# A gated linear recurrence whose next block's projection, convolution and split come ahead of the preceding block's scans, and whose gate products come together

## The chip, the cores and the metric

The kernel runs on one core of one Trainium2 chip. The metric is the device time of one execution in microseconds (us); several runs are taken and their median is compared.

## What is computed

The reference is one layer of an encoder trunk with four parallel branches, applied to two sequences (prompt and sample) of 1024 tokens and 1024 channels. Everything is float32. The change touches one branch, a gated linear recurrence (LRU) over 512 channels, in four blocks of 128. Cut to that branch:

```python
def rglru_branch(u, gate, conv_w, conv_b, w_a, b_a, w_x, b_x, lam):
    xc = centred_dwconv(u.astype(f32), conv_w.astype(f32)) + conv_b.astype(f32)
    xb = xc.reshape(bsz, L, LRU_BLOCKS, LRU_BLOCK_W)
    for d, rev in enumerate((False, True)):
        r = jax.nn.sigmoid(jnp.einsum('blhi,hij->blhj', xb, w_a[d].astype(f32)).reshape(bsz, L, LRU_W) + b_a[d].astype(f32))
        i = jax.nn.sigmoid(jnp.einsum('blhi,hij->blhj', xb, w_x[d].astype(f32)).reshape(bsz, L, LRU_W) + b_x[d].astype(f32))
        log_a = -LRU_C * jax.nn.softplus(-lam[d].astype(f32)) * r
        drive = jnp.sqrt(-jnp.expm1(2.0 * log_a)) * (i * xc)
        _, h = lax.associative_scan(_linear_combine, (jnp.exp(log_a), drive), axis=1, reverse=rev)
        hs.append(h)
    return ((hs[0] + hs[1]) * jax.nn.silu(gate.astype(f32))).astype(u.dtype)
```

u and gate are columns of one input projection of the normalised input. The other branches are a gated linear attention (GLA), a gated delta rule (DeltaNet), in which a lower triangular matrix I + L is inverted for each head and direction, and a diagonal state space model (S5). Each branch's output is projected, weighed with a sigmoid gate of the input ("merge gate") and added; an output projection and a norm close the layer.

## The kernel before

Tiles are channel-major: 128 channels on the partitions, 1024 tokens along a row. A float32 product is made of three passes over exact splits: each operand is a hi and a lo part, the hi a cast on ScalarE, the lo a subtraction on GpSimd, and TensorE computes hi x hi, hi x lo and lo x hi. A projection of 128 columns is two halves of 512 tokens, each 8 x 3 = 24 matmuls of 128x512 into a PSUM bank of the kind pj.

Each sequence passes through stages: the DeltaNet projections, then the **LRU stage**, then GLA and S5, then the DeltaNet recurrence with the merge, then the output projection. In the LRU stage three kinds of work are emitted side by side by `weave`, which spreads each generator evenly over its number of steps: `cor`, the inverses of I + L for two pairs of heads (`dn_core1`, 30 steps), `lru`, the four LRU blocks (16 steps), and some ten merge gates (`early`, tile fg); in sequence 0 also the rotations of S5 (tiles E and rot). The eight PSUM banks are cut into pj=3, lr=2 (the LRU's gate products) and dn=3 (DeltaNet). A scheduler of the framework then orders each engine's instructions by priority, close to the order of emission; each engine takes its own in that order and waits for semaphores.

An LRU block (`lru_block`) goes: projection into the tile up, convolution by four VectorE steps over 128x1024 into xc, cast xh (ScalarE), remainder xl (GpSimd), split of the gate weights, half of the block's silu gate (tile sg) as cover, then for each direction d two gates r and i, each two halves of three matmuls into an lr bank that a sigmoid on ScalarE empties; i x xc on GpSimd; exp, tanh and square on ScalarE; a VectorE step on r, a square root, a product i x r and the scan of 128x1024 on VectorE. Both directions share nothing but xc; r, i and sg have two buffers each. The next block's projection is emitted when the scans of the block before have been.

`dn_core1` builds L (tiles sl and rl: additions on VectorE, an exp on ScalarE, products with k k^T), writes its 32x32 diagonal blocks to DRAM (lan_d), reads them back one block per partition, and inverts them by 31 steps of two VectorE instructions (tm, then sl): here called the **lane solve**. The result goes through lan_d again, and 64- and 128-wide products on TensorE (tile dn) put the blocks together. There are two solves in each sequence, one per pair of heads; the stage's first half holds the first, its second half the other.

Every instruction is issued by a small helper and so has the same line, L54, in the profile: go by the tiles' names.

Of the kernel before, what the change touches and what calls it, by code (L numbers as in the profile page):

```python
# [17 lines left out]
T = 1024  # L18
# [15 lines left out]
def tile_hybrid_trunk(ctx: ExitStack, tc: tile.TileContext, A):  # L34
# [10 lines left out]
    class Line:  # L45
        """an engine that, while line[0] is set, takes its work in the order of the program"""
# [32 lines left out]
    def weave(*gens):  # L79
        """emit generators side by side, each spread evenly over its number of steps"""  # L80
# [8 lines left out]
    def after(i, j):  # L89
        """of one engine's instructions, i goes after j"""  # L90
# [35 lines left out]
    # ---------------------------------------------------------------- constants  # L126
# [5 lines left out]
    # ------------------------------------------------------- small helpers (DVE)  # L132
# [73 lines left out]
    def wcols(wp, src, k0, kt, c0, m):  # L206
        """columns c0:c0+m of rows 128 * (k0:k0+kt): list over k of (hi, lo) [128, m]"""
# [12 lines left out]
    def mm3_steps(out, ws, xs):  # L220
        """out[m, n] = sum_k w[k].T x[k], three float32r passes of the exact split; a step for each k"""
# [24 lines left out]
    # DRAM scratch  # L246
# [12 lines left out]
    # ================================================================ sequences  # L259
# [41 lines left out]
    def proj_tok(xn, wp, src, c0, toks, evac):  # L301
        """token-major: out[tok, 256 cols]"""
# [13 lines left out]
    def gate_steps(xn, wp, c0, out):  # L316
        """out = silu(projection block)"""
# [28 lines left out]
        # columns 0:48 the hi, 64:112 the lo part: one pass of the hi of xn carries both  # L346
# [25 lines left out]
    # ----------------------------------------------------------------- DeltaNet  # L372
# [1286 lines left out]
```

## Time and profile before

| | us |
|---|---|
| median of 3 runs | 3234.07 (3233.86 to 3234.88) |
| profiled execution, its span | 3238.6 |
| TensorE busy in it | 2991.5 (92%) |
| VectorE busy | 1986.7 (61%) |
| ScalarE busy | 1250.0 (39%) |
| GpSimd busy | 1077.0 (33%) |

The span is the profiled execution's time from its first instruction to its last; no other time of that execution is known, and it is one execution. Busy time counts instructions that run, so what is left of the span is an engine's idle time. "Clock" is the share of its full clock, 2.4 GHz, that TensorE was granted. A row of the form "PE lr <- ACT xh" says that a matmul into a tile lr waited for ScalarE's result xh.

### The profile page before, as it was taken

The numbers are of one execution on the slowest core, as the hardware profiler recorded it, in microseconds if no ns is written. First come the engines' busy times: TensorE is split into PE (matmuls) and PEld (weight loads), VectorE is DVE, ScalarE is ACT, GpSimd is POOL, SyncE is SP. The second block draws the span as 40 slices with busy tenths as digits, with TensorE's granted clock in tenths as the row PEclk, the third lists the DMA queues.
The fourth block names the chain that finished last, engine by engine and source line by source line (L and its number), as shares of the span: only waits on it lengthen the run. The fifth ranks groups of instructions, "written<-read, shape, count | busy, mean of one in ns | idle before, by whom it ended". The sixth has DMA issues, their size and how long they took to land. (4 is left out here: it accounts for less than half of the span.)

```text
span 3238.6 us, 42921 instructions
## 1 busy us (share of the span) xinstructions
PE 2991.5 (92%) x15642; PEld 2490.3 (77%) x15642; DVE 1986.7 (61%) x3941; ACT 1250.0 (39%) x1948; POOL 1077.0 (33%) x851
## 2 busy tenths in 40 slices
PE   6898879899899999999999988989989999999998
PEld 4666667779798787778778866777879788788877
DVE  6998885721767556565655367672266744656645
ACT  4333555532323244332254355652232324433223
POOL 2267643421334223111343333442133422321123
PEclk9999889999999999999999998999999999999999
DMA  5234525331323346654453342533123334565343
GB/s 106 93 131 141 175 78 160 92 121 27 91 85 108 115 142 195 199 195 127 160 174 112 104 129 81 157 88 121 40 79 99 109 101 158 182 205 184 114 151 124
DMA packets 397812, 409.04 MB, mean 126 GB/s; under 512 B 93184, under 2 KB 290848, under 8 KB 397600
## 3 DMA queue, kind: packets, MB, share of 16 engines
q1 hardware_dynamic: 397600, 406.29, 40.3%
q8 instruction: 123, 2.02, 0.3%
q14 instruction: 89, 0.73, 0.1%
HBM read 298.48 MB, written 107.71 MB: 125 GB/s over the span
## 5 line engine op out<-in xcount | busy, mean ns | idle before, releaser
L54 PE MATMUL pj<-xn,hi 128*128 128x512 f32 x4352 | 1402.0, 402 | 19.8 <-DVE misc L54 4.3
L54 POOL TENSOR_TENSOR lo<-raw,hi 128x512 fp32r<-128x512 f32 x432 | 612.9, 1423 | 1529.3 <-ACT hi L54 1405.6
L54 PEld LDWEIGHTS pj<-xn,hi 128*128 128x128 f32 x4352 | 824.0, 192 | 205.4 <-issue 15.2
L54 PE MATMUL pj<-xn,lo 128*128 128x512 f32 x2176 | 868.4, 399 | 2.4 <-POOL lo L54 2.4
L54 ACT CAST hi<-raw 128x512 fp32r<-128x512 f32 x432 | 264.7, 618 | 785.3 <-PE pj L54 512.6
L54 PEld LDWEIGHTS pj<-xn,lo 128*128 128x128 f32 x2176 | 417.8, 192 | 100.7 <-issue 7.4
L54 ACT ACT_TABLE_LOAD x184 | 236.1, 1283 | 96.8 <-DVE Ab L54 50.4
L54 PE MATMUL pj<-hi,xn 128*128 128x256 f32 x1024 | 263.1, 346 | 3.4 <-DVE vt L54 3.4
L54 PE MATMUL pj<-yh,hi 128*128 128x512 f32 x576 | 237.4, 412 | 5.1 <-DVE mg L54 3.9
L54 PEld LDWEIGHTS pj<-hi,xn 128*128 128x128 f32 x1024 | 230.3, 266 | 4.2 <-DVE vt L54 3.8
L54 PE MATMUL pj<-yh,lo 128*128 128x512 f32 x576 | 226.0, 392 | 0.0
L54 PE MATMUL pj<-yl,hi 128*128 128x512 f32 x576 | 225.4, 391 | 0.4 <-DVE yl L54 0.4
L54 PE MATMUL pj<-lo,xn 128*128 128x256 f32 x512 | 176.4, 347 | 0.0
L54 DVE TENSOR_TENSOR sg<-sg,pj 128x512 f32<-128x512 f32 x128 | 87.5, 684 | 100.8 <-PE pj L54 83.0
L54 PEld LDWEIGHTS pj<-lo,xn 128*128 128x128 f32 x512 | 135.3, 266 | 0.4
L54 PE MATMUL pj<-hi,mh 128*128 128x512 f32 x384 | 124.0, 399 | 7.0 <-ACT mh L54 4.1
L54 PEld LDWEIGHTS pj<-yh,hi 128*128 128x128 f32 x576 | 109.0, 189 | 24.6 <-DVE mg L54 4.5
L54 PEld LDWEIGHTS pj<-yh,lo 128*128 128x128 f32 x576 | 108.4, 188 | 23.8
L54 PEld LDWEIGHTS pj<-yl,hi 128*128 128x128 f32 x576 | 109.1, 189 | 19.2 <-DVE yl L54 1.1
L54 ACT ACTIVATE fg<-pj,bmg 128x512 f32<-128x512 f32 x112 | 76.6, 686 | 81.9 <-PE pj L54 47.3
L54 DVE TENSOR_TENSOR_SCAN w<-E,v 64x512 f32<-64x512 f32 x64 | 100.3, 1568 | 0.9
L54 DVE TENSOR_TENSOR yl<-yr,yh 128x512 fp32r<-128x512 f32 x80 | 60.3, 763 | 63.2 <-ACT yh L54 62.9
(380 smaller groups left out, 4608.8 us busy)
## 6 DMA issues: line engine op xcount, KB each, us to landing
raw<-in_w_in_dram SPq DMA_DIRECT2D x176, 256.0 KB, 2.9
raw<-in_w_merge_gate_dram SPq DMA_DIRECT2D x128, 256.0 KB, 3.3
sl<-rows_d SPq DMA_DIRECT2D x128, 256.0 KB, 6.6
gs_d<-fg SPq DMA_DIRECT2D x112, 256.0 KB, 3.3
sg<-gs_d SPq DMA_DIRECT2D x112, 256.0 KB, 2.9
sl<-qkv_d SPq DMA_DIRECT2D x40, 512.0 KB, 5.0
raw<-in_w_branch_dram SPq DMA_DIRECT2D x64, 256.0 KB, 3.4
yr<-ysp SPq DMA_DIRECT2D x64, 256.0 KB, 3.1
```

What stands on the lines that cost most here:

```text
L54: i = f(*a, **kw)
```

## The change

`lru_block` becomes `lru_all`, one generator for all four blocks, in three parts. `front(b)` is a block's projection, convolution and split, now by halves of 512 tokens, and its gate weights. `products(b)` makes all eight gate tiles of a block (two directions, r and i, two halves) one after the other, and the two products i x xc. `scans(b)` holds the block's silu gate, and for each direction exp, tanh, square, square root and scan. They are emitted as front 0, then for each b: products b, front b + 1, scans b. The square gets a tile of its own (a2; it lay in up), sg has one buffer, and the weave counts 18.4 steps for the LRU. `conv` takes its width from its output. All else in the diff is removed comments.

```diff
     def conv(out, up, cw, bias=None):
+        n = out.shape[1]
         if bias is None:
-            ts(V, out, up[:, 0:T], cw[:, 0:1], None, ALU.mult)
+            ts(V, out, up[:, 0:n], cw[:, 0:1], None, ALU.mult)
         else:
-            ts(V, out, up[:, 0:T], cw[:, 0:1], bias, ALU.mult, ALU.add)
+            ts(V, out, up[:, 0:n], cw[:, 0:1], bias, ALU.mult, ALU.add)
         for j in range(1, 4):
-            stt(out, up[:, j:j + T], cw[:, j:j + 1], out, ALU.mult, ALU.add)
+            stt(out, up[:, j:j + n], cw[:, j:j + 1], out, ALU.mult, ALU.add)
...
-    def lru_block(s, b, xn, wp, pl):
...
+    def lru_all(s, xn, wp, pl):
+        two = ("r", "i")
         wt = lambda shape, tag, dt=F32: pl.tile(shape, dt, tag=tag, name=nm(tag), bufs=2 if tag in two else 1)
+        def front(b):
+            up = wt([128, T + 4], "up")
+            conv_in(xn, wp, up, LRU_X + b * 128)
+            yield 1
+            xc = wt([128, T], "xc")
+            xh, xl = wt([128, T], "xh", F32R), wt([128, T], "xl", F32R)
+            cb = lru_cb[:, b:b + 1]
+            for sl in HALVES:
+                conv(xc[:, sl], up[:, sl.start:sl.stop + 3], lru_cw[:, b], cb)
+                S.copy(xh[:, sl], xc[:, sl])
+                tt(G, xl[:, sl], xc[:, sl], xh[:, sl].bitcast(F32), ALU.subtract)
...
+            hi, lo = split_tile(pl, 512, srcs, 512, "lw", 1, 1)
+            return xc, xh, xl, hi, lo
+        def products(b, xc, xh, xl, hi, lo):
+            r, ig = ([wt([128, T], t_) for _ in range(2)] for t_ in two)
+            for d in range(2):
+                for gi, (dst, bias) in enumerate(((r[d], lru_ba), (ig[d], lru_bx))):
+                    mi = slice((gi * 2 + d) * 128, (gi * 2 + d + 1) * 128)
+                    for sl in HALVES:
+                        p = bank("lr")
+                        for n, (a, x) in enumerate(((hi, xh), (hi, xl), (lo, xh))):
+                            mm(p, a[:, mi], x[:, sl], start=(n == 0), stop=(n == 2))
+                        act(dst[:, sl], p, AF.Sigmoid, bias=bias[:, d, b:b + 1])
                     yield 0.4
+                tt(G, ig[d], ig[d], xc, ALU.mult)
+            return r, ig
+        def scans(b, r, ig):
+            sg = wt([128, T], "sg")
+            gate = gate_steps(xn, wp, LRU_G + b * 128, sg)
...
+            half()
+            for d in range(2):
+                j = d * 4 + b
+                a = wt([128, T], "a")
+                act(a, r[d], AF.Exp, scale=sp8n[:, j:j + 1])
+                act(r[d], r[d], AF.Tanh, scale=sp8[:, j:j + 1])
+                a2 = wt([128, T], "a2")
...
+                half()
+                if d == 0:
+                    yield 1
+            run(gate)
+            tt(G, ig[0], ig[0], ig[1], ALU.add)
+            tt(V, sg, ig[0], sg, ALU.mult)
+            put_y(sg, s, 0, b)
+            yield 1
+        new = yield from front(0)
+        for b in range(4):
+            got = yield from products(b, *new)
+            if b < 3:
+                new = yield from front(b + 1)
+            yield from scans(b, *got)
...
-                lru = chain(*(lru_block(s, b, xn, wp, pl) for b in range(4)))
+                lru = lru_all(s, xn, wp, pl)
                 cor = chain(*(dn_core1(s, p, pr, cpl) for p in range(2)))
-                todo = [(30, cor), (16, lru), *early(s, NP[s][2], 0.15, xn, wp, fp)]
+                todo = [(30, cor), (18.4, lru), *early(s, NP[s][2], 0.15, xn, wp, fp)]
```

The rows that follow are the engines' orders of instructions. On TensorE, sequence 0, before the change: pj468 and pj470 belong to merge gates (before pj468 stand the two halves of block 0's gate, 24 matmuls each), lr432 and lr433 are the first gate products of block 0.

```order
L54 MATMUL pj468_3277<-xn0_6_98,hi466_3272 128x512 x2
L54 MATMUL pj468_3277<-xn0_6_98,lo467_3273 128x512
L54 MATMUL pj468_3277<-xn0_7_99,hi466_3272 128x512 x2
L54 MATMUL lr432_3097<-xh416_3025,hi419_3030 128x512
L54 MATMUL lr433_3102<-xh416_3025,hi419_3030 128x512
L54 MATMUL pj468_3277<-xn0_7_99,lo467_3273 128x512
L54 MATMUL pj470_3305<-xn0_0_92,hi463_3266 128x512 x2
L54 MATMUL pj470_3305<-xn0_0_92,lo464_3267 128x512
L54 MATMUL pj470_3305<-xn0_1_93,hi463_3266 128x512 x2
```

After the change, the same place: pj464 and pj465 are the two halves of block 1's projection, lr425 is block 0's first product.

```order
L54 MATMUL pj464_3233<-xn0_7_99,hi462_3228 128x512 x2
L54 MATMUL pj464_3233<-xn0_7_99,lo463_3229 128x512
L54 MATMUL pj465_3259<-xn0_0_92,hi459_3222 128x512 x2
L54 MATMUL pj465_3259<-xn0_0_92,lo460_3223 128x512
L54 MATMUL pj465_3259<-xn0_1_93,hi459_3222 128x512 x2
L54 MATMUL pj465_3259<-xn0_1_93,lo460_3223 128x512
L54 MATMUL lr425_3046<-xh416_3021,hi419_3036 128x512
L54 MATMUL pj465_3259<-xn0_2_94,hi459_3222 128x512 x2
L54 MATMUL pj465_3259<-xn0_2_94,lo460_3223 128x512
L54 MATMUL pj465_3259<-xn0_3_95,hi459_3222 128x512 x2
L54 MATMUL lr425_3046<-xl417_3022,hi419_3036 128x512
L54 MATMUL lr425_3046<-xh416_3021,lo420_3037 128x512
```

The first product has moved up: 30 matmuls of block 1's projection stand between block 0's projection (and eight dn products) and it, where 24 of each of two gate halves and 23 of a merge gate stood. Block 1's projection is now here instead of behind the scans.

On VectorE, sequence 0, before: xc566 is block 1's convolution, sl477 and tm are the lane solve (the 13th to 15th of its 31 steps are among these rows), i484 is block 0's scan, sg421 its output.

```order
L54 TENSOR_TENSOR tm529_3622<-sl476_3363,sl477_3364 128x247
L54 TENSOR_TENSOR E881_5525<-E881_5525,tm894_5572 128x4x64
L54 TENSOR_TENSOR sl477_3364<-sl477_3364,tm529_3622 128x13x19
L54 TENSOR_TENSOR tm530_3625<-sl476_3363,sl477_3364 128x252
L54 TENSOR_SCALAR xc566_3785<-up520_3555,lru_cw_407,lru_cb_412 128x1024
L54 TENSOR_TENSOR sl477_3364<-sl477_3364,tm530_3625 128x14x18
L54 TENSOR_TENSOR sg421_3036<-i454_3220,sg421_3036 128x1024
L54 SCALAR_TENSOR_TENSOR xc566_3785<-up520_3555,lru_cw_407,xc566_3785 128x1024
L54 TENSOR_TENSOR tm531_3628<-sl476_3363,sl477_3364 128x255
L54 SCALAR_TENSOR_TENSOR xc566_3785<-up520_3555,lru_cw_407,xc566_3785 128x1024
L54 TENSOR_TENSOR sl477_3364<-sl477_3364,tm531_3628 128x15x17
L54 SCALAR_TENSOR_TENSOR xc566_3785<-up520_3555,lru_cw_407,xc566_3785 128x1024
```

After: xc477 is block 1's convolution, in halves; i424 is the product i x r and the scan of block 0's second direction; sl495 and tm are the solve (its 6th and 7th step).

```order
L54 TENSOR_TENSOR tm501_3488<-sl494_3468,sl495_3469 128x156
L54 TENSOR_SCALAR xc477_3372<-up457_3218,lru_cw_407,lru_cb_412 128x512 x2
L54 TENSOR_TENSOR i424_3045<-i424_3045,r422_3043 128x1024
L54 TENSOR_TENSOR sl495_3469<-sl495_3469,tm501_3488 128x6x26
L54 SCALAR_TENSOR_TENSOR xc477_3372<-up457_3218,lru_cw_407,xc477_3372 128x512 x2
L54 SCALAR_TENSOR_TENSOR i424_3045<-a533_3636,i424_3045 128x1024
L54 TENSOR_TENSOR tm527_3618<-sl494_3468,sl495_3469 128x175
L54 SCALAR_TENSOR_TENSOR xc477_3372<-up457_3218,lru_cw_407,xc477_3372 128x512
L54 TENSOR_TENSOR tm886_5531<-E881_5516,rot_512 128x4x4
L54 SCALAR_TENSOR_TENSOR xc477_3372<-up457_3218,lru_cw_407,xc477_3372 128x512
L54 TENSOR_TENSOR sl495_3469<-sl495_3469,tm527_3618 128x7x25
L54 SCALAR_TENSOR_TENSOR xc477_3372<-up457_3218,lru_cw_407,xc477_3372 128x512
```

The convolution of block 1 has moved from the middle of the solve to its beginning, and lies in pieces between its steps.

On ScalarE, sequence 1, block 0, before: sl2805 is an exp of L, r2800 the first direction's r from the banks lr2801 and lr2802, a2811 the exp of the recurrence behind it.

```order
L54 ACTIVATE r2800_16045<-lr2801_16046,lru_ba_414 128x512
L54 ACT_TABLE_LOAD
L54 ACTIVATE sl2805_16087<-sl2805_16087 128x1024
L54 ACT_TABLE_LOAD
L54 ACTIVATE r2800_16045<-lr2802_16051,lru_ba_414 128x512
L54 ACT_TABLE_LOAD
L54 ACTIVATE a2811_16123<-r2800_16045,sp8n_503 128x1024
```

After: sl2803 and sl2808 are exps of L; i2792, r2790 and r2791 are sigmoids that empty banks (r2791 belongs to the second direction).

```order
L54 ACT_TABLE_LOAD
L54 ACTIVATE sl2808_16108<-sl2808_16108 128x1024
L54 ACT_TABLE_LOAD
L54 ACTIVATE i2792_16017<-lr2799_16056,lru_bx_417 128x512
L54 ACT_TABLE_LOAD
L54 ACTIVATE r2790_16015<-r2790_16015 128x1024
L54 ACT_TABLE_LOAD
L54 ACTIVATE r2791_16016<-lr2800_16062,lru_ba_414 128x512
```

The sigmoids that empty the banks now stand with an exp of L ahead of them, which waits for VectorE, and with four table loads and the first direction's square root (the row that reads and writes r2790) among them.

## Rows read from the trace of the kernel before

**Rows 1.** The page: its head and TensorE's busy time.

```profile
span 3238.6 us, 42921 instructions
...
PE 2991.5 (92%) x15642; PEld 2490.3 (77%) x15642; DVE 1986.7 (61%) x3941; ACT 1250.0 (39%) x1948; POOL 1077.0 (33%) x851
```

**Rows 2.** Windows of the two LRU stretches: busy us and instructions, clock, DMA.

```profile
334.00:720.00 386.00, 340.06 (x1832) 273.17 (x1833) 256.42 (x485) 198.26 (x275) 164.33 (x165) 0.92 0.42 127
...
1886.00:2251.00 365.00, 326.11 (x1778) 261.34 (x1778) 232.51 (x401) 195.62 (x268) 133.21 (x93) 0.93 0.40 121
```

**Rows 3.** TensorE's waits, 334 to 720 us: total us, times, longest.

```profile
PE lr L54 <- ACT xh L54: 17.9, 3, 7.1
...
PE dn L54 <- DMA sl<-lan_d: 6.7, 2, 4.9
...
PE lr L54 <- ACT r L54: 5.9, 2, 3.1
...
PE lr L54 <- POOL xl L54: 3.3, 2, 1.8
```

**Rows 4.** TensorE's waits, 1886 to 2251 us.

```profile
PE lr L54 <- ACT xh L54: 10.5, 2, 5.9
...
PE dn L54 <- DMA sl<-lan_d: 6.2, 2, 4.8
...
PE lr L54 <- ACT i L54: 5.2, 1, 5.2
...
PE lr L54 <- ACT r L54: 4.7, 1, 4.7
...
PE lr L54 <- POOL xl L54: 3.6, 2, 1.9
```

**Rows 5.** Timeline, TensorE, products behind a wait: start, duration, operation, [idle before].

```profile
552.40 0.50 PE L54 MATMUL lr<-xh,hi 128*128 128x512 f32 x1 [3.06 <-ACT r L54]
...
614.46 0.79 PE L54 MATMUL lr<-xh,hi 128*128 128x512 f32 x1 [5.20 <-ACT xh L54]
...
617.02 0.80 PE L54 MATMUL lr<-xl,hi 128*128 128x512 f32 x1 [1.77 <-POOL xl L54]
...
2147.95 0.80 PE L54 MATMUL lr<-xh,hi 128*128 128x512 f32 x1 [5.94 <-ACT xh L54]
...
2150.50 0.80 PE L54 MATMUL lr<-xl,hi 128*128 128x512 f32 x1 [1.76 <-POOL xl L54]
```

**Rows 6.** Windows behind two waits, and one at full clock.

```profile
552.00:557.00 5.00, 4.60 (x13) 3.64 (x14) 0.00 (x0) 4.94 (x6) 0.00 (x0) 0.66 0.33 105
...
614.40:621.60 7.20, 5.38 (x12) 3.95 (x13) 6.99 (x7) 4.82 (x9) 5.36 (x3) 0.50 0.22 71
...
621.80:629.00 7.20, 7.20 (x33) 5.83 (x32) 6.82 (x12) 6.46 (x8) 2.63 (x2) 1.00 0.14 37
```

**Rows 7.** Windows of the lane solves in the first halves.

```profile
354.60:462.00 107.40, 87.98 (x368) 71.07 (x367) 102.98 (x202) 61.47 (x71) 54.30 (x68) 0.89 0.43 127
...
1955.80:2007.00 51.20, 44.80 (x182) 35.84 (x180) 49.36 (x74) 22.24 (x28) 19.91 (x13) 0.90 0.23 69
```

**Rows 8.** Instructions of tile i: min/median/max ns, first and last start.

```profile
L54 POOL TENSOR_TENSOR i<-i,xc x16: 2358/2400/2923, 395.5 to 2186.2; 128x1024 f32<-128x1024 f32 x16
...
L54 DVE TENSOR_TENSOR i<-i,r x16: 1182/1225/2258, 398.7 to 2191.8; 128x1024 f32<-128x1024 f32 x16
...
L54 DVE TENSOR_TENSOR_SCAN i<-a,i x16: 2269/2292/3266, 399.9 to 2193.5; 128x1024 f32<-128x1024 f32 x16
```

**Rows 9.** Instructions of tile xc: a convolution step.

```profile
L54 DVE SCALAR_TENSOR_TENSOR xc<-up,lru_cw,xc x24: 1269/1279/1293, 362.8 to 2145.5; 128x1024 f32<-128x1024 f32 x24
```

**Rows 10.** Timeline at 614 us: lane solve on VectorE, subtraction on GpSimd.

```profile
614.33 0.42 DVE L54 TENSOR_TENSOR sl<-sl,tm 128x252 f32<-128x252 f32 x1
...
614.48 2.48 POOL L54 TENSOR_TENSOR xl<-xc,xh 128x1024 fp32r<-128x1024 f32 x1 [17.45 <-ACT xh L54]
...
614.78 2.55 DVE L54 TENSOR_TENSOR tm<-sl,sl 128x247 f32<-128x247 f32 x1
```

More of the change, by code (lines that the diff above doesn't have):

```diff
@@ L798, in norm_out @@
         put_y(y, *dst)
-    def lru_block(s, b, xn, wp, pl):
-        two = ("r", "i", "sg")
+    def lru_all(s, xn, wp, pl):
+        two = ("r", "i")
         wt = lambda shape, tag, dt=F32: pl.tile(shape, dt, tag=tag, name=nm(tag), bufs=2 if tag in two else 1)
-        up = wt([128, T + 4], "up")
-        conv_in(xn, wp, up, LRU_X + b * 128)
-        yield
-        xc = wt([128, T], "xc")
-        conv(xc, up, lru_cw[:, b], lru_cb[:, b:b + 1])
-        xh, xl = wt([128, T], "xh", F32R), wt([128, T], "xl", F32R)
-        S.copy(xh, xc)
-        tt(G, xl, xc, xh.bitcast(F32), ALU.subtract)
-        def srcs(raw):
-            v = raw[:, :512].rearrange("p (a d c) -> p a d c", a=2, d=2)
-            yield v[:, 0], A["lru_w_a"][0, :, b].rearrange("d i j -> i d j")
-            yield v[:, 1], A["lru_w_x"][0, :, b].rearrange("d i j -> i d j")
-        hi, lo = split_tile(pl, 512, srcs, 512, "lw", 1, 1)
-        sg = wt([128, T], "sg")
-        gate = gate_steps(xn, wp, LRU_G + b * 128, sg)
-        def half():
-            for _ in range(8):
-                next(gate, None)
-        half()
-        yield 0.4
-        hv = []
-        for d in range(2):
-            gts = []
-            for gi, bias in ((0, lru_ba), (1, lru_bx)):
-                r = wt([128, T], ("r", "i")[gi])
-                mi = slice((gi * 2 + d) * 128, (gi * 2 + d + 1) * 128)
-                for hf in range(2):
-                    sl = slice(hf * 512, (hf + 1) * 512)
-                    p = bank("lr")
-                    for n, (a, x) in enumerate(((hi, xh), (hi, xl), (lo, xh))):
-                        mm(p, a[:, mi], x[:, sl], start=(n == 0), stop=(n == 2))
-                    act(r[:, sl], p, AF.Sigmoid, bias=bias[:, d, b:b + 1])
-                gts.append(r)
-                if gi == 0:
-                    if d == 0:
-                        half()
-                        run(gate)
-                    yield 0.4
-            r, ig = gts
-            j = d * 4 + b
-            tt(G, ig, ig, xc, ALU.mult)
-            a = wt([128, T], "a")
-            act(a, r, AF.Exp, scale=sp8n[:, j:j + 1])
-            act(r, r, AF.Tanh, scale=sp8[:, j:j + 1])
-            a2 = wt([128, T + 4], "up")[:, 0:T]
-            act(a2, a, AF.Square)
-            stt(r, a2, 1.0, r, ALU.add, ALU.mult)
-            act(r, r, AF.Sqrt)
-            tt(V, ig, ig, r, ALU.mult)
-            if d == 0:
-                V.tensor_tensor_scan(ig, a, ig, 0.0, ALU.mult, ALU.add)
-            else:
-                V.tensor_tensor_scan(ig[:, ::-1], a[:, ::-1], ig[:, ::-1], 0.0, ALU.mult, ALU.add)
-            hv.append(ig)
-            yield
-        tt(G, hv[0], hv[0], hv[1], ALU.add)
-        tt(V, sg, hv[0], sg, ALU.mult)
-        put_y(sg, s, 0, b)
-        yield 0.01
@@ new lines, in front, with srcs @@
+        def front(b):
[9 more added lines that the diff above has]
+                tt(G, xl[:, sl], xc[:, sl], xh[:, sl].bitcast(F32), ALU.subtract)
+            def srcs(raw):
+                v = raw[:, :512].rearrange("p (a d c) -> p a d c", a=2, d=2)
+                yield v[:, 0], A["lru_w_a"][0, :, b].rearrange("d i j -> i d j")
+                yield v[:, 1], A["lru_w_x"][0, :, b].rearrange("d i j -> i d j")
+            hi, lo = split_tile(pl, 512, srcs, 512, "lw", 1, 1)
+            return xc, xh, xl, hi, lo
@@ new lines, in scans, with half @@
+        def scans(b, r, ig):
+            sg = wt([128, T], "sg")
+            gate = gate_steps(xn, wp, LRU_G + b * 128, sg)
+            def half():
+                for _ in range(8):
+                    next(gate, None)
+            half()
[5 more added lines that the diff above has]
+                a2 = wt([128, T], "a2")
+                act(a2, a, AF.Square)
+                stt(r[d], a2, 1.0, r[d], ALU.add, ALU.mult)
+                act(r[d], r[d], AF.Sqrt)
+                tt(V, ig[d], ig[d], r[d], ALU.mult)
+                h = ig[d]
+                if d == 0:
+                    V.tensor_tensor_scan(h, a, h, 0.0, ALU.mult, ALU.add)
+                else:
+                    V.tensor_tensor_scan(h[:, ::-1], a[:, ::-1], h[:, ::-1], 0.0, ALU.mult, ALU.add)
+                half()
+                if d == 0:
+                    yield 1
[4 more added lines that the diff above has]
+            yield 1
```

## The prediction

> **What bounds the kernel now.** The page's head comes first [rows 1]: TensorE (PE) is busy for 2991.5 of 3238.6 us, 92%, and no other engine passes 61%. The time is therefore TensorE's work plus its idle time, and a change that leaves its work alone can only move idle time and clock. The windows by stage come second [rows 2]. The stage in which the LRU blocks, the lane solve and early merge gates are woven is 334 to 720 us for sequence 0 and 1886 to 2251 us for sequence 1. TensorE is busy 340 of 386 us and 326 of 365 us there, at a mean granted clock of 0.92 and 0.93: 46 + 39 = 85 us idle in these two stretches, a third of the 247 us of the whole span. Here the change can act.
>
> The list of waits, for TensorE in each stretch, comes third [rows 3, 4]. The gate products (tile lr) wait for xh, r, i and xl: 17.9 + 5.9 + 3.3 = 27.1 us in sequence 0 and 10.5 + 5.2 + 4.7 + 3.6 = 24.0 us in sequence 1, together 51.1 us. The first products after the lane solve (dn, for the DMA that brings lan_d back) wait 6.7 and 6.2 us. The reader should see why: TensorE takes its instructions in order, and xh and xl come out of a chain (projection, four VectorE steps, a cast on ScalarE, a subtraction on GpSimd) for which it has too little other work in front.
>
> Last the windows around three waits [rows 5, 6]. After the wait of 5.20 us that ends at 614.46 us the clock is 0.50, half of 2.4 GHz: 12 matmuls begin in 7.20 us, where the next 7.20 us at 1.00 take 33. So full pace is 0.218 us a matmul, a half projection of 24 matmuls 5.2 us, and the 21 that are missing are 4.6 us, of which 1.8 is the wait for xl that falls in the window: 2.8 us is the price of the slow clock. At 552.40 us, after 3.06 us, 13 begin in 5.00 us at 0.66, ten short of 23 at full pace: 2.2 us. I put the clock at 2.4 us for each wait of several microseconds, an estimate from these two; nine such waits make 22 us. Waits and clock of the gate products together are a ceiling of 51 + 22 = 73 us.
>
> **What the change does, part by part.** Instruction counts, by the orders of the two programs: TensorE 13574 rows in both; VectorE 3943 to 3975, from the convolution in halves; ScalarE 1902 to 1908; GpSimd 856 to 864; SP 1554 in both, so no DMA is added. The halves work on the same columns, and no row shows one: if the cut adds 10% to the 64 halves of 0.64 us that a step of 1.28 us [rows 9] makes, that is 4 us on VectorE, of which the windows below say where it counts. Outside the two stretches the orders agree except around sequence 0's output projection, which I put at 0, within 4 us. TensorE's instructions stay. What changes is what stands between a block's projection and its products.
>
> *Blocks 0* have no preceding scans. In sequence 0, 71 matmuls of 128x512 stand between the end of their projection and their first product (both halves of the block's gate and 23 of a merge gate); after the change 30 (of block 1's projection), in sequence 1 likewise. That is 41 x 0.218 = 9.0 us less cover. Against it, products need only one half of the convolution, 2.6 us sooner by half of four steps of at most 1.28 us [rows 9], and the waits for r and i that follow in the old order (5.9 - 3.06 = 2.8 us in sequence 0; 4.7 and 5.2 in sequence 1) lose their place, since two directions no longer follow each other with an exp between. Before, these blocks wait 5.6 + 2.8 = 8.4 and 9.9 us; after, I find about 10 and 11. I take 0 as the sum for both, from -8 (cover lost, nothing regained) to +8 (the r and i waits go).
>
> *First half of sequence 0, block 1 and lane solve.* VectorE is busy 102.98 of 107.40 us from 354.60 to 462.00 [rows 7]: here VectorE sets when the solve ends, and nothing that TensorE does ahead matters. The VectorE rows in the section on the change show block 1's convolution going in at the sixth step of the solve, where it stood at the fourteenth, and with it block 1's first scan group comes ahead of the solve's end: a step on r of about the product's size, 1.23, the product itself, 1.23, and a scan of 2.29 [rows 8], 4.7 us, of which the idle 4.4 us of that window takes about half. Twelve more matmuls (2.6 us) stand ahead of the solve's first product. Block 1's 7.1 + 1.5 us of waits then become wait for lan_d: 0, from -3 to +3.
>
> *First half of sequence 1.* The solve has a window of its own, 1955.80 to 2007.00, VectorE 49.36 of 51.20 us busy [rows 7]. The matrix L is complete some 3 us later after the change (its exp stands behind evictions), but 3.4 us less other VectorE work lies inside the solve, so its end stays, while 32 more matmuls stand ahead of its first product: 32 x 0.218 = 7.0 us. Range 2 to 11.2; the upper end is all that waits there, 4.5 + 1.9 for xh and xl and 4.8 for lan_d [rows 4].
>
> *Second halves, blocks 2 and 3.* Here TensorE is ahead of its inputs only at single places: 3.06 + 5.20 + 1.77 us in sequence 0 and 5.94 + 1.76 us in sequence 1 [rows 5], 17.7 us, with 2.2 + 2.8 + 2.4 = 7.4 us of clock. For block 3, three half projections (15.7 us) stood between projection and product and 5.2 to 5.9 us were lacking, so 21 to 22 us are needed. After the change six stand there in sequence 1 (31 us) and about as many in sequence 0, since the block's projection stands ahead of the preceding block's gate projection and scans. 31 is over 22 by 9 us, which also covers what VectorE puts in between. So 17.7 + 7.4 = 25.1 us go.
>
> *What it adds.* Eight product tiles now go through two lr banks with little between them. Each bank is freed by a sigmoid on ScalarE, whose order has the lane solve's exps and table loads among these sigmoids. No row shows this arrangement; the nearest is the wait for r at 552.40, 3.06 us, with 2.2 us of clock, and the farthest 5.2 us for i [rows 4]. I take one such wait of 4 us in each sequence, 8 us; bounds 0 and 8 blocks x 7 us = 56. Nobody but TensorE waits behind it, and with TensorE everything.
>
> **The sum.** 0 + 0 + 7.0 + 25.1 - 8 = 24.1 us, against the profiled execution's span of 3238.6, which gives 3214.5. The runs' median is 3234.07, 4.5 us (0.14%) below that span; from it, 3234.1 - 24.1 = **3210 us**. What a measurement can tell from no change is 0.2%, 6.5 us.
>
> **Rivals.** *All the waits of blocks 1 to 3 go*: 51.1 less the 18.3 of blocks 0 is 32.8 us, and five clocks at 2.4 make 12: 45 us, 3189 us. For it speaks the longer cover; against it VectorE's 96% in the first halves, which more cover cannot hurry. Chance 0.12.
>
> *VectorE and GpSimd delay the solve, and the waits come back as waits for lan_d.* The rows at 614 us show what stands against the change: while GpSimd's subtraction of 2.48 us runs, VectorE's solve step of 128x247 takes 2.55 us where the step just before, of 128x252, took 0.42 [rows 10]. After the change a block's two GpSimd products i x xc (2.40 each, [rows 8]) follow its eight products and fall into the solve, as does the subtraction of the next block. If each costs VectorE some 2 us more, the solve of each of four pairs ends 6 us later, and 4 x 6 = 24 us is all of the gain: 3234 us, no change. Against it: each of these GpSimd steps also ran beside a solve or its neighbours before. Chance 0.16. The Trainium skill states a rule that bears on this ("SBUF — State Buffer", section "SBUF: two separate sides"): the port pair that VectorE and GpSimd share is an exclusive lock, and of a VectorE step with two SBUF inputs and a GpSimd step that reads SBUF the one that starts first blocks the other for its whole length. By that rule, the trace agrees with 2.55 against 0.42 us, and every GpSimd step moved into the solve is paid in full: this rival's 3234 us, against 3210 if such steps only change places.
>
> *Slower: the lr banks become a queue.* In ScalarE's order after the change (the last rows in the section on the change) an exp of L, which waits for VectorE, stands between the sigmoids that free the two banks. If that holds TensorE in each of the eight blocks as i held it once (5.2 us and 1.8 of clock), it costs 56 us, and takes back the whole 45: +11, 3245 us. It decides from six and a half blocks on. For it: two banks, eight tiles; against it: of the waits before, only four lie at a bank's sigmoid. Chance 0.16.
>
> **How the numbers follow.** The forecast has 0.56, 3210 us, its own range 3198 to 3222 from the bounds of blocks 0 (8), of sequence 1's first half (5) and of the added waits (8), not all at once. Faster by over 0.2% are forecast and first rival, 0.68; within 0.2% the second, 0.16; slower the third, 0.16. The range reaches to 3190 and 3238, which leaves out half of the first rival (below 3190) and most of the third, some 0.2.
>
> **What would show it.** In the trace after: waits of lr for xh in blocks 2 and 3 gone, those in the windows of blocks 0 still some 8 to 10 us; waits for lan_d as long or longer in sequence 0 and shorter in sequence 1; clock above 0.95 in the second halves; TensorE's busy time about 10 to 15 us less from the clock alone, its count the same. Wrong would be: waits of lr for r or i (a bank's sigmoid) of over 20 us together, which is the third rival; waits for lan_d of over 25 us together, the second.

## The result: slower by 0.77%

The changed kernel takes 3254.62 us (median of 4 runs, 3252.35 to 3267.56) against 3234.48 us of the kernel before on the same chip; the ratio is 1.0077, 95% interval 1.0055 to 1.0099. I had forecast 3210 us. The profiled execution of the changed kernel is the longest of its four (3267.56 us), so its sums may be some 13 us too long; the difference of the two profiled spans, 27.2 us, is 7 us more than that of the medians.

The page of the changed kernel, head and TensorE's row, and its windows of the two LRU stretches, which answer to [rows 1, 2]:

```profile
span 3265.8 us, 42992 instructions
...
PE 3008.2 (92%) x15642; PEld 2499.3 (77%) x15642; DVE 2000.7 (61%) x3973; ACT 1249.1 (38%) x1954; POOL 1079.7 (33%) x859
```

```profile
334.00:733.00 399.00, 346.11 (x1832) 275.93 (x1833) 259.27 (x501) 198.75 (x278) 161.75 (x168) 0.91 0.40 123
...
1898.00:2276.50 378.50, 330.96 (x1777) 264.65 (x1778) 239.21 (x417) 193.32 (x270) 135.49 (x97) 0.92 0.39 117
```

Both stretches hold the same matmuls (1832 each; 1777 and 1778) and have grown from 386 to 399 and from 365 to 378.5 us: 26.5 of the 27.2 us between the two spans. Of that 15 to 16 us are idle time (45.9 to 52.9, 38.9 to 47.5) and 11 us are busy time (340.06 to 346.11, 326.11 to 330.96), with a granted clock of 0.91 and 0.92 where it was 0.92 and 0.93. TensorE's waits in these stretches (total us, times, longest), sequence 0 and then sequence 1, which answer to [rows 3, 4]:

```profile
PE lr L54 <- ACT xh L54: 13.1, 2, 6.7
PE dn L54 <- DMA sl<-lan_d: 12.7, 4, 6.5
PE lr L54 <- ACT i L54: 10.2, 2, 6.8
PE pj L54 <- DVE sg L54: 6.9, 3, 3.1
PE lr L54 <- ACT r L54: 6.6, 3, 3.9
```

```profile
PE dn L54 <- DMA sl<-lan_d: 17.5, 3, 7.6
PE lr L54 <- ACT i L54: 10.4, 3, 5.8
PE pj L54 <- DVE sg L54: 4.7, 2, 3.1
...
PE lr L54 <- ACT r L54: 3.1, 2, 1.9
...
PE lr L54 <- ACT xh L54: 2.1, 1, 2.1
PE lr L54 <- POOL xl L54: 2.0, 1, 2.0
```

The waits the change was counted on to shorten did shrink: xh and xl from 35.3 to 17.2 us over the kernel. Three others grew more: r and i, that is, a full lr bank, from 15.7 to 30.2; lan_d from 12.8 to 30.1; and pj for sg, a gate half whose VectorE product is late, from 4.1 to 13.5. The net is 23 us more. All other rows of the list together fell by 12 us, so that the whole list grew by 11 (237.6 to 248.5 us).

Three places show how. ScalarE in the changed kernel, block 1 of sequence 0 (timeline: start, duration, operation, idle before it):

```profile
447.70 0.68 ACT L54 ACTIVATE i<-lr,lru_bx 128x512 f32<-128x512 f32 x1
448.40 1.28 ACT L54 ACT_TABLE_LOAD   x1
455.82 1.06 ACT L54 ACTIVATE r<-r 128x1024 f32<-128x1024 f32 x1 [6.14 <-DVE r L54]
456.90 1.28 ACT L54 ACT_TABLE_LOAD   x1
458.19 0.69 ACT L54 ACTIVATE i<-lr,lru_bx 128x512 f32<-128x512 f32 x1
```

TensorE, same place:

```profile
458.93 0.80 PE L54 MATMUL lr<-xh,hi 128*128 128x512 f32 x1 [6.85 <-ACT i L54]
```

The row at 455.82 is the square root of the recurrence. It waits 6.14 us for a VectorE step on r, which comes at 454.57 among the steps of the lane solve. The sigmoid at 458.19, whose bank has long been full, stands behind it, and TensorE's next product behind that: 6.85 us.

But a wait for VectorE is not needed. Of the ten waits for r and i, five (14.1 us) lie behind an instruction of ScalarE that waits for VectorE, twice the square root and three times an exp of L. Four (14.9 us) lie behind a ScalarE that does not idle at all, but goes through exps, square roots and table loads; the tenth, of 1.27 us, lies behind a cast of xh and a table load. The longest of the four, block 0 of sequence 1, on ScalarE and then on TensorE:

```profile
1945.87 1.28 ACT L54 ACT_TABLE_LOAD   x1
1947.16 1.06 ACT L54 ACTIVATE sl<-sl 128x1024 f32<-128x1024 f32 x1
1948.24 1.28 ACT L54 ACT_TABLE_LOAD   x1
1949.53 0.69 ACT L54 ACTIVATE i<-lr,lru_bx 128x512 f32<-128x512 f32 x1
```

```profile
1950.27 0.80 PE L54 MATMUL lr<-xh,hi 128*128 128x512 f32 x1 [5.78 <-ACT i L54]
```

The third place is the second lane solve of sequence 0. Its first and last step and what follows, VectorE:

```profile
604.83 0.21 DVE L54 TENSOR_TENSOR tm<-sl,sl 128x31 f32<-128x31 f32 x1 [7.76 <-DMA sl<-lan_d]
...
656.28 0.22 DVE L54 TENSOR_TENSOR sl<-sl,tm 128x31 f32<-128x31 f32 x1
667.99 1.25 DVE L54 STREAM_TRANSPOSE sl<-sl 128x1024 f32<-128x1024 f32 x1 [11.49 <-DMA sl<-lan_d]
```

The same rows of the kernel before:

```profile
587.22 1.21 DVE L54 TENSOR_TENSOR tm<-sl,sl 128x31 f32<-128x31 f32 x1
...
631.56 0.22 DVE L54 TENSOR_TENSOR sl<-sl,tm 128x31 f32<-128x31 f32 x1
```

The solve starts 17.6 us later, lasts 51.7 instead of 44.6 us, and ends 24.7 us later, at 656.5. At 661.5 us what comes of it is next in TensorE's order, and TensorE waits 6.50 us:

```profile
668.00 0.69 PE L54 MATMUL dn<-sl,LE 128*64 128x64 f32 x8 [6.50 <-DMA sl<-lan_d]
```

The late solve is not all of this wait. The way through lan_d, from the solve's end to the transpose, takes 11.49 us, and 6.16 before (in sequence 1, 11.99 and 6.17). The queue that issues the DMAs (SPq, a row an issue), changed kernel:

```profile
656.52 0.32 SPq L597 DMA_DIRECT2D lan_d<-sl  x1
656.89 0.45 SPq L1221 DMA_DIRECT2D tin<-tin_d  x1
657.39 0.90 SPq L1222 DMA_DIRECT2D E<-rot_d  x1
658.34 0.48 SPq L1223 DMA_DIRECT2D tout<-tout_d  x1
...
660.01 1.56 SPq L631 DMA_DIRECT2D sl<-lan_d  x2
...
662.63 1.88 SPq L631 DMA_DIRECT2D sl<-lan_d  x2
```

The kernel before:

```profile
631.80 0.34 SPq L596 DMA_DIRECT2D lan_d<-sl  x1
634.47 1.81 SPq L630 DMA_DIRECT2D sl<-lan_d  x4
```

tin, E and tout are loads for S5, of the next stage. Behind the second solve of either sequence the changed kernel issues them between the write of lan_d and its reading back; the kernel before issues none there. TensorE came to the lane product 5.0 us after the solve's end in both sequences, so with the 6.2 us of before it would have waited some 1.2 us where it waited 6.50 and 6.99: an estimate of 11 of the 30.1 us of lan_d that go with the longer way through lan_d and not with the solve. No run moves these loads, so what they cost in the end is not shown. The solve's late start is a wait too: ahead of it VectorE stood idle for 7.76 us for lan_d (8.53 in sequence 1), and did not before.

### The profile page after: what moved, and what is told of

The parts are those of the page before. It is cut to its first block, busy times and chain, and to the rows that moved or that the text cites. A ratio compares the mean times of both kernels' runs of the same rounds, so it can differ in the third digit from the quotient of the medians.

```text
span 3265.8 us, 42992 instructions
## 1 busy us (share of the span) xinstructions
PE 3008.2 (92%) x15642; PEld 2499.3 (77%) x15642; DVE 2000.7 (61%) x3973; ACT 1249.1 (38%) x1954; POOL 1079.7 (33%) x859
## 5 line engine op out<-in xcount | busy, mean ns | idle before, releaser
L54 PE MATMUL pj<-xn,hi 128*128 128x512 f32 x4352 | 1410.5, 404 | 29.3 <-DVE sg L54 13.5
L54 POOL TENSOR_TENSOR v<-E,w 128x512 f32<-128x512 f32 x32 | 54.5, 1704 | 132.8 <-DVE w L54 92.7
```

The costliest lines, as they stand in the source:

```text
L54: i = f(*a, **kw)
```

## The experiments

Each ratio is to the kernel before, run beside it on the same chip (its medians were 3229 to 3231 us there, and 3234.48 us beside the changed kernel). The waits are sums of rows of the list of waits over the whole kernel, in us.

| kernel | ratio (95% interval) | r, i | xh, xl | lan_d | sg |
|---|---|---|---|---|---|
| before | 1 | 15.7 | 35.3 | 12.8 | 4.1 |
| changed | 1.0077 (1.0055 to 1.0099) | 30.2 | 17.2 | 30.1 | 13.5 |
| e5 halves alone | 0.9991 (0.9981 to 1.0002) | 10.3 | 28.5 | 20.1 | 3.4 |
| e8 front ahead, products by direction | 1.0025 (1.0017 to 1.0034) | 14.6 | 32.4 | 20.9 | 11.6 |
| e1 products together, front late | 1.0051 (1.0038 to 1.0063) | 43.1 | 38.1 | 10.7 | 2.3 |
| e2 sigmoids first | 1.0037 (1.0024 to 1.0051) | 10.1 | 8.9 | 54.1 | 14.7 |
| e3 solve emitted early | 1.0126 (1.0112 to 1.0140) | 41.2 | 21.0 | 12.3 | 14.9 |
| e7 three lr banks | 1.0025 (1.0016 to 1.0034) | 25.9 | 8.6 | 20.6 | 21.4 |
| e16 gate early, sequence 1 | 1.0091 (1.0077 to 1.0105) | 28.3 | 20.3 | 32.5 | 8.9 |
| e17 e16 with three lr banks | 1.0039 (1.0024 to 1.0053) | 21.4 | 7.3 | 32.2 | 18.2 |
| e19 e2 with short convolution | 1.0014 (1.0003 to 1.0024) | 17.4 | 0.0 | 44.1 | 7.0 |
| e20 more cover | 1.0090 (1.0075 to 1.0105) | 42.1 | 11.7 | 16.7 | 12.4 |
| e21 e2 with more cover | 1.0031 (1.0021 to 1.0042) | 15.9 | 7.2 | 34.7 | 15.3 |
| e22 before with more cover | 1.0044 (1.0029 to 1.0058) | 14.1 | 14.2 | 25.1 | 3.2 |
| e13 before, rotations behind | 0.9970 (0.9960 to 0.9980) | 19.3 | 32.3 | 12.2 | 1.9 |
| e14 e2, rotations behind | 0.9982 (0.9971 to 0.9992) | 6.9 | 5.0 | 48.5 | 22.3 |
| e18 e5, rotations behind | 0.9956 (0.9944 to 0.9969) | 16.6 | 26.1 | 19.2 | 3.0 |
| e23 e2, e7, more cover, rotations | 0.9977 (0.9966 to 0.9989) | 10.0 | 5.0 | 19.2 | 12.7 |

**Which part of the change costs: e1, e8, e5.** The change has three parts, halves, front ahead, products together; with the changed kernel these four make a square, all with the halves. The square is not clean. e5 is built on the kernel before, so that its silu gate still stands ahead of and among a block's products, and sg's buffers, a2's place and the weave's steps are the old ones too. And in e8 the next front passes ahead of the second direction's scan only.

```diff
 e1, on the changed kernel
-        new = yield from front(0)
         for b in range(4):
+            new = yield from front(b)
             got = yield from products(b, *new)
-            if b < 3:
-                new = yield from front(b + 1)
             yield from scans(b, *got)
 e8, on the changed kernel
-            got = yield from products(b, *new)
+            yield from products(b, 0, *new, r, ig)
...
+            yield from scans(b, 0, r, ig, sg, gate)
+            yield from products(b, 1, *new, r, ig)
             if b < 3:
                 new = yield from front(b + 1)
-            yield from scans(b, *got)
+            yield from scans(b, 1, r, ig, sg, gate)
 e5, on the kernel before
-        conv(xc, up, lru_cw[:, b], lru_cb[:, b:b + 1])
-        S.copy(xh, xc)
-        tt(G, xl, xc, xh.bitcast(F32), ALU.subtract)
+        for sl in HALVES:
+            conv(xc[:, sl], up[:, sl.start:sl.stop + 3], lru_cw[:, b], lru_cb[:, b:b + 1])
+            S.copy(xh[:, sl], xc[:, sl])
+            tt(G, xl[:, sl], xc[:, sl], xh[:, sl].bitcast(F32), ALU.subtract)
```

Expected of e1: 

> The changed kernel, with a block's front (projection, convolution, split) emitted behind the preceding block's scans again; its eight gate products stay together and its convolution in halves. Bank theory (the loss comes from sigmoids that stand on ScalarE behind an exp or square root that waits for VectorE, so that the two lr banks stay full): the waits of lr for r and i stay at 25 to 35 us, the waits for xh and xl come back from 17 to about 35 us, time 3265 to 3275 us. Late-solve theory (the loss comes from fronts and products that pass ahead of the lane solves on TensorE and VectorE, so that the cover is used up before the solve ends): the waits for lan_d fall from 30 to 10 to 15 us and those of pj for sg from 13 to about 4, xh comes back all the same, time 3240 to 3248 us.

Expected of e8: 

> The changed kernel with the gate products direction by direction, as before the change: products and scan of the first direction, products of the second, then the next block's front, then the second direction's scan. Bank theory: the waits for r and i fall to about 16 us as before the change, those for xh and xl stay near 17, time 3236 to 3244 us. Late-solve theory: the front still passes ahead, the waits for lan_d stay at 25 to 30 us, time 3245 to 3255 us.

Expected of e5: 

> The kernel before with the convolution, cast and remainder in halves of 512 tokens and nothing else changed. If xh being ready half a convolution sooner is worth something where TensorE waits for it: the waits for xh fall from 28 us by about 2.6 us in each of five places, 10 to 13 us, time 6 to 12 us below the kernel before. If VectorE sets the pace in these halves (the late-solve theory): the waits only change their name, time within 6 us of the kernel before.

The halves alone are worth nothing that can be told from zero (0.9991). From there, products together, with what else differs, cost 0.60 points (1.0051), the front's move as e8 has it 0.34 (1.0025), and both 0.86 (1.0077): within the intervals they add up, and the changed kernel's interval overlaps that of e1. The waits of e1, over the whole kernel, show what the products' part costs:

```profile
PE lr L54 <- ACT xh L54: 37.3, 6, 10.7
...
PE lr L54 <- ACT r L54: 30.4, 11, 5.3
...
PE lr L54 <- ACT i L54: 12.7, 5, 4.3
PE dn L54 <- DMA sl<-lan_d: 10.7, 5, 4.0
```

43.1 us for r and i, against 10.3 in e5. Here the bank theory is right that r and i stay, and its time (3265 to 3275) is far off. What the late-solve theory said came: 3247.76 us, lan_d at 10.7, sg at 2.3 and xh back. In e8 it is the other way round: r and i at 14.6 and 3237.16 us are what the bank theory gave, and lan_d, at 20.9, is under the late-solve theory's 25 to 30; but xh and xl come back to 32.4 us, which neither had. Against e5 what is new there is sg, 11.6 against 3.4. So neither theory holds for both parts.

**Is it the bank: e2 and e7.** e2 lets no exp of a block pass the last sigmoid of its products on ScalarE, e7 cuts the banks anew.

```diff
 e2, on the changed kernel
-                        act(dst[:, sl], p, AF.Sigmoid, bias=bias[:, d, b:b + 1])
+                        last_sig[:] = [act(dst[:, sl], p, AF.Sigmoid, bias=bias[:, d, b:b + 1])]
...
-                act(a, r[d], AF.Exp, scale=sp8n[:, j:j + 1])
+                e = act(a, r[d], AF.Exp, scale=sp8n[:, j:j + 1])
+                if d == 0:
+                    after(e, sig)
 e7, on the changed kernel
-                banks(st, pj=3, lr=2, dn=3)
+                banks(st, pj=3, lr=3, dn=2)
```

Expected of e2: 

> The changed kernel with one order more on ScalarE: a block's first exp goes after the last sigmoid of that block's products, so no exp or square root of the block stands ahead of a sigmoid that empties a bank. Bank theory: the waits of lr for r and i fall from 30 us to under 12, time 3235 to 3242 us. Late-solve theory: the scans start later and lie deeper in the lane solve, the waits for lan_d and sg grow by what the others lose, time 3250 to 3260 us.

Expected of e7: 

> The changed kernel with three lr banks and two dn banks (before: two and three). Bank theory: the third bank takes one more product while a sigmoid stands behind an exp or square root, the waits for r and i fall from 30 us to 10 to 20. Whether this is gain or only moves the waits to lan_d decides between the theories: time 3235 to 3245 us if banks were the cause in themselves, 3245 to 3260 us if VectorE sets when the lane solve ends.

e2 does what it is to do: r and i fall from 30.2 to 10.1, xh and xl to 8.9. Its time is 3245.06 us, between the theories: 0.40 of the 0.77 points are gone. Of the 28.4 us that these waits lost, 24.0 came back in lan_d, which goes from 30.1 to 54.1 us; its first lane product in each sequence:

```profile
475.51 0.80 PE L54 MATMUL dn<-sl,LE 128*64 128x64 f32 x10 [15.68 <-DMA sl<-lan_d]
```

```profile
2011.55 0.70 PE L54 MATMUL dn<-sl,LE 128*64 128x64 f32 x8 [15.68 <-DMA sl<-lan_d]
```

TensorE gains at the banks and loses at the next wait. e7 gives 0.52 points back (3240.23 us, as the bank theory said), but not from where it said: r and i are down by 4 us only, to 25.9 and not to 10 to 20, xh, xl and lan_d by 18, and sg is up by 8.

**Is the solve late for want of VectorE: e19, e13, e14.** e19 leaves three of the four VectorE steps of each convolution of e2 out, 3.9 us a block, so it computes something else. e13 and e14 order the S5 rotations of sequence 0 behind its first lane solve and start to emit them in the middle of the stage (0.5 in place of 0.1), in the kernel before and in e2.

```diff
 e19, on e2
-                conv(xc[:, sl], up[:, sl.start:sl.stop + 3], lru_cw[:, b], cb)
+                ts(V, xc[:, sl], up[:, sl], lru_cw[:, b, 0:1], cb, ALU.mult, ALU.add)
 e13, e14
-            V.memset(E[:, 0, :, 0:1], 1.0)
+            e = V.memset(E[:, 0, :, 0:1], 1.0)
+            if solve:
+                after(e, solve[-1])
...
-            tt(V, xv, xv, tv, ALU.subtract)
+            solve.append(V.tensor_tensor(xv, xv, tv, ALU.subtract))
...
-                    todo.append((8, s5_rot(rot, pool("s5e", 1, stack=st)), 0.1))
+                    todo.append((8, s5_rot(rot, pool("s5e", 1, stack=st)), 0.5))
```

Expected of e19: 

> The changed kernel with the sigmoids first on ScalarE, and three of the four VectorE steps of each LRU convolution left out, so it computes another recurrence: its input is scaled and not convolved. That is 3.9 us of VectorE less in each of eight blocks and nothing else. VectorE-bound solves: lan_d waits fall from 54 us by 12 to 25 us, time 12 to 25 us below the 3245 us of the kernel with the sigmoids first. If the solves end when they do for another reason (a DMA, the exps of L on ScalarE): lan_d stays within 6 us of 54, time within 6 us.

Expected of e13: 

> The kernel before with the S5 rotations of sequence 0 (tiles E and rot, some 10 us of VectorE inside the first lane solve and as much ahead of it) ordered on VectorE behind the first lane solve. VectorE-bound halves: the first solve of sequence 0 ends 10 us or more sooner, the waits for xh and lan_d of that half (15 us) shrink by 8 or more, and those of the second half grow by 0 to 10; time 10 us below to 3 us above the kernel before. If VectorE doesn't set the pace: no wait of the first half changes by over 2 us.

Expected of e14: 

> The changed kernel with the sigmoids first on ScalarE, and the S5 rotations behind the first lane solve of sequence 0 on VectorE. VectorE-bound halves: the one wait of 15.7 us for lan_d in the first half of sequence 0 falls to 6 us or less, as the solve ends 10 us sooner; sequence 1, which has no rotations, keeps its 15.7 us; time 5 to 10 us below the kernel with the sigmoids first alone. If anything but VectorE sets it: the 15.7 us stay.

e19: lan_d falls by 10 us and the time by 0.23 points, some 7 us, of 31 us of VectorE left out: VectorE has a part in the late solve, not all of it. The part is in the first halves: the solves there last 50.57 and 45.60 us, against 59.93 and 54.53 in e2. In the second halves, where no convolution lies in e2's solve, the solves last 38 us in both and the waits stay (6.88 and 6.38 us, against 6.08 and 6.50). There the way through lan_d takes 10.5 us in both kernels, against 6.2 before: in e2 the queue of DMAs stops for 2.9 us, at a store of a merge gate that waits for its sigmoid, with reads of lan_d behind it. e13 and e14 gain, but not where I expected. Windows ahead of the stage, e13 and before, over the same 1214 matmuls:

```profile
0.00:303.50 303.50, 248.59 (x1214) 191.37 (x1214) 261.47 (x654) 121.50 (x206) 96.43 (x77) 0.96 0.41 116
```

```profile
0.00:320.00 320.00, 254.87 (x1214) 195.55 (x1214) 282.15 (x734) 121.74 (x206) 152.09 (x156) 0.93 0.40 116
```

The 16.5 us are won in the projections of DeltaNet: the scheduler had put rotations there, 56 us on GpSimd and 21 on VectorE. (By its ratio e13 gains 0.30%, some 10 us, in all.) In e14's LRU stage hardly anything is won: the lane products of the half in question still wait 9.82 and 4.93 us, against 15.68. The step of that expectation (the solve ends sooner, so the wait shrinks) failed, since TensorE came there sooner too.

**Emission, cover and the gate: e3, e16, e17, e20, e21, e22.** Each shifts other work against the solve.

```diff
 e3, on the changed kernel
-                todo = [(30, cor), (18.4, lru), *early(s, NP[s][2], 0.15, xn, wp, fp)]
+                todo = [(34, cor), (18.4, lru), *early(s, NP[s][2], 0.15, xn, wp, fp)]
 e16 and e17, on the changed kernel and on e7, in products
+            if s == 1:
+                sg = wt([128, T], "sg")
+                gate = gate_steps(xn, wp, LRU_G + b * 128, sg)
+                for _ in range(8):
+                    next(gate, None)
...
+                    if gate and d == gi == 0:
+                        run(gate)
 e20, e21, e22, on the changed kernel, on e2 and on the kernel before
-    NP = ((2, 0, 11, 4, 2, 3, 3), (0, 0, 10, 4, 2, 4, 2))
+    NP = ((2, 0, 13, 2, 2, 3, 3), (0, 0, 12, 2, 2, 4, 2))
```

Expected of e3: 

> The changed kernel with the weave's steps of the DeltaNet generator counted as 34 instead of 30, so that its work, the lane solves among it, is emitted up to an eighth of the stage earlier. Late-solve theory: the waits for lan_d fall from 30 us to under 15, the last pair's solve starts 10 us or more sooner, time 3235 to 3245 us. Bank theory: the waits for r and i stay at 30 us, those for lan_d were a consequence, time 3250 to 3258 us.

Expected of e16: 

> The changed kernel, in sequence 1 alone (its tiles fit there) with a block's silu gate projected ahead of and among its products, as before the change, instead of with its scans. If the front's move costs what shows as waits of pj for sg (a gate half whose VectorE product lies behind the scans and the lane solve holds a pj bank): in sequence 1's stretch these waits fall from 4.7 us to under 1, lr waits for xh and xl (4.1 us) go to 0 with the longer cover, and the time falls by 4 to 9 us, to 3240 to 3249 us; sequence 0 as in the changed kernel. If sg is a symptom of a late solve: lan_d grows by as much, time within 3 us of the changed kernel's.

Expected of e17: 

> The same with three lr banks and two dn banks. If bank queue and gate's place are the two costs and add up: the gain of the third bank (0.52% on the changed kernel) and that of the gate together, 3228 to 3236 us, no slower than the kernel before by over 0.15%. If VectorE's late solve takes them back: 3238 us or more.

Expected of e20: 

> The changed kernel with two of the four merge gates that stand at the end of each LRU stage woven into the stage instead (the sum of gates is the same), so that 43 to 83 more matmuls stand ahead of the last lane solve's first product. Cover theory (TensorE reaches the lane products too soon because the change moved other work ahead, and the four gates behind them run without a wait): lan_d in the second halves falls from 18 us to under 6, time 3240 to 3248 us. If the chain to the lane products only moves with TensorE's order: within 4 us of the changed kernel's 3254.

Expected of e21: 

> The same with the sigmoids first on ScalarE. Cover theory: of the 54 us of waits for lan_d the 20 us of the second halves go, those of 15.7 us in each first half stay, as hardly a matmul more stands ahead of them; time 3228 to 3236 us. Otherwise 3240 to 3248.

Expected of e22: 

> The kernel before with the same two gates woven in. It has only 2.4 us of waits for lan_d in its second halves, so cover theory: little to gain there, time within 5 us of the kernel before, with the waits for xh of blocks 2 and 3 somewhat shorter.

e3 brings lan_d down to 12.3 us and is the slowest of all, 1.0126, far from both theories: r and i go to 41.2. e16 brings sg down to 8.9 and isn't faster (3262.53 us): in sequence 1, where its edit is, sg fell from 4.7 to 3.1 us only and lan_d rose from 17.5 to 21.1, so the late gate halves alone are not the cost. e17 gives no more than e7 did. e20 brings lan_d from 30.1 to 16.7 and keeps its time within the intervals, with i alone at 30.1:

```profile
PE lr L54 <- ACT i L54: 30.1, 7, 9.5
PE dn L54 <- DMA sl<-lan_d: 16.7, 6, 6.0
```

Of the 16.7 us 14 are still in the second halves, where I expected under 6. e21 takes 19 us of lan_d away for 0.06 points, within its interval. In e22 the waits listed fall by 11 us in all and the time rises by 0.44%, outside what I expected. The whole list of its waits does not fall (237.6 to 238.2 us), since others grew; of the 8.3 us between the spans, 7.6 are TensorE's busy time, over the same 15642 matmuls, at a granted clock of 0.963 against 0.968. So cover ahead of the lane products was not the cause that it looked like.

**Edits put together: e18, e23.** e18 is e5 with the rotations of e13; e23 puts e2, e7, e20's gates and the rotations together.

Expected of e18: 

> The kernel before with the convolution in halves and the S5 rotations behind the first lane solve, the two edits that didn't lose: if they add up 0.9961 of the kernel before, some 3218 us; if the rotations take the place that the halves freed, 0.997, as the rotations alone.

Expected of e23: 

> The changed kernel with all that gave something back: sigmoids first, three lr banks, more cover, and the S5 rotations behind the first lane solve. If the costs found are all there is, it comes to 3205 to 3218 us, below the halves with the rotations behind (0.9956); if the waits only change places it stays at 3222 to 3232 us.

e18 is the fastest, 3217.72 us, 0.9956: two edits that add up as expected, without the change's reordering. e23, 3222.43 us, is 0.23% faster than before but not than e18, whatever is taken off the banks: at the near end of the range for waits that only change places. 19 us of lan_d and 42 us of other waits of dn (15 in the kernel before) remain in it.

## Why the prediction was wrong

Both signs that I had named for being wrong came: waits for r and i of 30.2 us, over 20, and for lan_d of 30.1 us, over 25. The clock in the second halves, for which I had said above 0.95, was 0.93 and 0.94, and TensorE's busy time grew by 16.7 us instead of falling.

*Blocks 0* were read right: about 10 and 11 us of waits foreseen, 11.6 (6.44, 1.80, 3.32) and 10.6 (1.27, 1.64, 5.78, 1.86) measured.

*First halves.* For sequence 0 I had 0; the five waits around block 1 and the lane products went from 17.7 to 20.0 us. For sequence 1 I had a gain of 7.0; its waits for xh, xl and lan_d there went from 11.3 to 11.7, and one of 2.3 us for rl, just behind the lane product, came on top. The step "so its end stays, while 32 more matmuls stand ahead of its first product" failed: the solve, 1955.84 to 2005.92 before, is 1977.79 to 2025.01 after, 19 us later, of which some 12 us were lost in sequence 0, ahead of this stage.

*Second halves* is the step that failed most. "So 17.7 + 7.4 = 25.1 us go" holds for xh: blocks 2 and 3 have no such wait left, and their waits for r and i are 7.7 us (0.88, 3.90, 2.93). But the term ends at the product. What comes next on TensorE was put at nothing without a reason: the lane products of the second solve, which before waited 1.14 and 1.31 us and now wait 18.5 (6.50, 2.14, 6.99, 2.85), and gate halves, none before and now 9.1 us (1.28, 3.15, 1.52, 3.15). In place of 17.7 us less, these waits together went from 20.2 to 35.3 us, 15 more. Part of that, the longer way through lan_d, comes from an engine that the prediction left out: it counted that no DMA is added, and did not ask where in the queue the reads of lan_d would stand. The wait changed its name, as my own second rival said, but not by its mechanism. What GpSimd adds to the solves did not grow: summing, over the 62 steps of each solve, what a step takes beyond its shortest in the eight solves of the two traces, I get 48.8 us before and 40.5 after, of which 46.3 and 37.8 are in steps that ran beside a GpSimd instruction. The Trainium skill's rule of the exclusive lock ("SBUF — State Buffer", section "SBUF: two separate sides") agrees with single rows, as [rows 10], but what it prices did not grow, so it does not explain the loss.

*What it adds* was mis-sized. I took one wait of 4 us in each sequence for the banks; r and i grew by 14.5 us, and in e1, without the front's move, stand 33 us over e5. The place I named for the third rival (an instruction that waits for VectorE between the sigmoids on ScalarE) was right for about half of these waits; the other half stand behind exps, square roots and table loads of a ScalarE that did not wait. Its price, 7 us in each of eight blocks, was too high, and "takes back the whole 45" joined it to the first rival's gain, which never came; the +11 us it gave is nearest to the measured +20 by two errors that cancel.

Shown is: products together (e1) and the front's move as e8 has it each make the kernel slower; a sigmoid behind a waiting square root, or behind ScalarE's other work, holds TensorE; and what e2 takes from TensorE's waits at the banks comes back in good part as a wait for lan_d, as what e3 and e20 take from lan_d comes back at the banks. Not shown is what sets the sum, nor what the gate's new place has in either cost. VectorE's load has a part (e19), the bank's number too (e7); more cover, an earlier gate in sequence 1 or an earlier solve have not. The place of the reads of lan_d in the queue of DMAs is a cause that the traces show and no run tests. That the front's move costs 0.26 (0.77 less the 0.51 of e1) to 0.34 points by way of late gate halves is argued from e8's waits only, and e16 speaks against it.

## What to carry to other kernels

When work moves on an engine that takes its instructions in order, price the wait that comes next behind the removed one, and the one after; a term that ends at the shortened wait counts a gain that may be handed on. Before results are made together into a few PSUM banks, read the order of the engine that empties them: what stands there between two evictions closes the banks, whether it waits for a third engine or only takes its own time, as table loads do. A queue that issues DMAs is such an order too: a read that work waits for can stand behind loads for a later stage. And split a change into its parts on the chip: here four kernels showed that both parts cost, which two theories of waits did not.

## What the runs showed that I had not expected

Work of one stage, emitted early because its inputs were ready, cost another stage more than its own: the S5 rotations on GpSimd and VectorE delayed the DeltaNet projections by 16.5 us in the profiled execution. TensorE's wait for GpSimd's product there (cr for dcv) is 11.8 us in the kernel before and 1.1 in e13, in the list of waits of the first 334 and 320 us.
